# A hybrid block on one core: x also as its transpose, the norm moved behind the projections, two chunks streamed first

## The chip, the cores and the metric

The kernel runs on 1 core of a Trainium2 chip. The metric is the device time of one execution in microseconds. A core has a matmul engine (TensorE, PE in the rows; its weight loads are PEld), a vector engine (VectorE, DVE), an activation engine (ScalarE, ACT), a general engine (GpSimd, POOL) and a queue that issues all transfers of this kernel (SyncE, SPq). Each runs its own list of instructions in order, and semaphores tie the lists together.

## The reference, cut to what matters

```
h = rmsnorm(x, g_mix_pre)                    # x: 1024 tokens x 1024; per token 1/rms, per column g
proj = h @ w_in                              # qa ka va gate (4 heads x 128), beta alpha (4+4), qb kb vb (8 heads x 64)
out_a = gated_deltanet(...)                  # conv over tokens, silu, l2norm; per chunk of 64 tokens
                                             #   t_inv = inverse(I + a), then a recurrence over chunks
out_b = dilated_attention(qb, kb, vb, rel_bias)
x = x + rmsnorm(concat(out_a, out_b) @ w_out, g_mix_post)
h = rmsnorm(x, g_ffn_pre)
out = x + rmsnorm((silu(h @ w_gate) * (h @ w_up)) @ w_down, g_ffn_post)
```

All arrays are float32. Since rmsnorm scales a token by one number r, `(x * r * g) @ w` is `r * ((x * g) @ w)`.

## The kernel before

The work is written as strands (Python generators, one for each task). A recording layer, the Weaver, runs them against its own table of costs and writes the instructions of each engine in the order in which they come up; every instruction therefore has the line of that one call, L267, and rows are read by tiles and shapes. On the chip the order is fixed and each engine waits where its operands are late.

A float32 product is made of three matmuls in a faster 32-bit form: both operands are split into a high part (a cast) and a low part (the rest), and `mm3` adds hi·hi, hi·lo and lo·hi in one PSUM bank. So every operand costs a cast (mostly ACT) and a subtraction (mostly DVE) before PE can use it.

Stage one (to about 300 us) works as follows. `norm_in` (L1171) loads a tile `xt` of 128 tokens, squares it on ACT with a sum (`junk`, `ss`), forms r on DVE and POOL (`n_m`, `n_r`), scales the tile by r and g on DVE, transposes it on PE (8 transposes into banks `tp`, 64 in all) and splits the result into `hTh` and `hTl`, the transposed activations. `load_w` (L625) loads the weight chunks `wr` of `w_in` in the sequence of `ORDER` (two transfers of 256 KB for a chunk of 128 columns), and `prep_w` splits them into `w`. `main` (L1132) is the strand of the projections and has the lowest priority: what it does fills PE whenever nothing else is due. Its first item is bv0 (`proj_v`, vb of four heads with beta and alpha: per token tile 24 matmuls of 264 columns, 192 in all), then k0, q0, k1 and so on: `proj_half` makes 24 matmuls of 512 columns for half of the tokens into one of two banks `pj`, and a sink reads the bank out and gives it back. `raw_sink` (L1110) copies k, q and v to `raw` on ACT. From there `post_k`, `post_q` and `post_v` do the convolution (four DVE passes, `yc`) and the rest, `intra` (L954) the products of a head inside its chunks (`pm<-kq` on PE, two groups of 64-column matmuls per head), `inverse` the triangular inverses by 31 steps on DVE, and `solve` (L1073), once per head, finishes them with four groups of small matmuls on PE (`pm<-uz`, `pm<-B,zz`, twice `pm<-attnT,B`). There are two banks `pm`.

After that come the recurrence and the attention with the last projections between them (300 to 500 us), the output projection `pw` (to about 640 us) and the feed-forward part (`bank`).

Of the kernel before, what the change touches and what calls it, by code (L numbers as in the profile page):

```python
# [21 lines left out]
P = 128  # L22
# [24 lines left out]
AHEAD = 2  # L47
SWITCH = 170.0
BREATH = 200.0
ORDER = "bv0,k0,q0,k1,q1,k2,q2,k3,q3,bq0,bv1,bk0,v0,v1,v2,v3,bq1,bk1,bq2,bk2,bq3,bk3,gate0,gate1,gate2,gate3"  # L50
# [471 lines left out]
def block_kernel(ctx: ExitStack, tc: tile.TileContext, a, out):  # L522
# [77 lines left out]


# [23 lines left out]
    def load_w():  # L625
        for item in order:
            for c in chunks(item):
                z = []
                for i in range(2):
                    wr = yield rawS.get([P, 4, P], F32, name="wr")  # L630
                    yield SY.dma_start(wr[:], a["w_in"][c][:, 4 * i:4 * i + 4, :])
                    z.append(wr)
                w.spawn(prep_w(c, z), 1)
            ev_w0.fire()

    ev_w0 = Event()

    def prep_w(c, raw):
# [7 lines left out]
        for i, (wr, wh, wl) in enumerate(zip(raw, hi, lo)):  # L646
# [11 lines left out]
        wts[c] = hi, lo  # L658
        loaded[c].fire()

# [11 lines left out]
    def proj_qk(c0, m, ev):  # L672
        scale = 0.125 if c0 == 16 else None
# [15 lines left out]
    def proj_v(m):  # L689
# [6 lines left out]
        def sink(t, ps):  # L696
            vs = yield outS.get([P, 4, 2, 64], F32R, name="vs")
            yield from split(vs[:, :, 0, :], vs[:, :, 1, :], ps[:, 0:256].rearrange("p (h d) -> p h d", h=4))
            if not m:
                yield A.copy(bp[:, :, t], ps[:, 256:WB])  # L700
            pj.put(ps)
# [3 lines left out]
        evs = []  # L705
        for t in range(NT):
            yield ev_ht[t]
            ps = yield pj.get([P, n], F32, name="pj")
# [10 lines left out]
            evs.append(w.spawn(sink(t, ps), 1))  # L719
        if not m:  # L720
            w.spawn(beta_alpha(evs), 2)
    def gate(*hs):
        def sink(h, hf, ps):
            z = yield gstS[h // 2, hf].get([P, 512], F32, name="gst")
            yield Either(A.copy(z[:], ps[:]), V.tensor_copy(z[:], ps[:]))
# [40 lines left out]
    ev_ht = [Event() for _ in range(NT)]  # L766
# [28 lines left out]
    def load_consts():  # L795
        yield ev_ht[3]
# [156 lines left out]

    def intra(h):  # L954
# [5 lines left out]
        for i, (m_in, lhs) in enumerate(((mD, trir), (mDT, tgtr))):  # L960
            rh = yield pk.get([P, 2 * NT, 64], F32R, name="rhd", bufs=1)
            yield G.tensor_tensor(rh[:], g2[:, h, :].bitcast(F32).unsqueeze(2).broadcast_to([P, 2 * NT, 64]),
                                  m_in[:].unsqueeze(1).broadcast_to([P, 2 * NT, 64]), ALU.mult)
# [12 lines left out]
            yield G.tensor_tensor(dst, dst, m_in[:].unsqueeze(1).broadcast_to([P, NT, 64]), ALU.mult)  # L976
# [6 lines left out]
        kq = kqs[h]  # L983
        for b in range(2):
            yield After(kq[:])
            kk = yield pm.get([P, 4, 2, 64], F32, name="pm")
            ops = []
# [4 lines left out]
            yield ops  # L992
# [27 lines left out]
    def inverse(evs):  # L1020
# [46 lines left out]
        for q in range(4):  # L1067
            w.spawn(solve(q, a21, uz, B, gs), 3, MARGIN, PACE)

    ev_g_out = [Event() for _ in range(GH)]  # L1070
    ev_gs = {(q, b): Event() for q in range(GH) for b in range(2)}

    def solve(q, a21, uz, B, gs):  # L1073

        sl = slice(q * 8, q * 8 + 8)
        yield After(a21[:], uz[:], B[:])
        zp = yield pm.get([P, 8, 32], F32, name="pm")
        yield [mm(zp[o:o + 32, u, :], a21[o:o + 64, q * 8 + u, :], uz[o:o + 64, q * 8 + u, :])
               for u in range(8) for o in (0, 64)]
        zz = yield pv.get([P, 8, 64], F32, name="zz", bufs=2)  # L1080
        yield G.memset(zz[:], 0.0)
        for o in (0, 64):
            yield V.tensor_tensor(zz[o:o + 32, :, 32:64], zp[o:o + 32, :, :],
                                  rk[o:o + 32, q, :].unsqueeze(2).broadcast_to([32, 8, 32]), ALU.mult)
        pm.put(zp)
        t2 = yield pm.get([P, 8, 32], F32, name="pm")
        yield [mm(t2[o:o + 64, u, :], zz[o:o + 32, u, :], B[o:o + 32, q * 8 + u, 0:32])
               for u in range(8) for o in (0, 64)]
# [3 lines left out]
        for b in range(2):  # L1092
            gg = yield pm.get([P, 4, 2, 64], F32, name="pm")
            ops = []
            for k in range(4):
                u = q * 8 + b * 4 + k
                for c in range(2):
                    o = c * 64
                    r = attnT[o:o + 64, u, :, :]
                    ops.append(mm(gg[o:o + 64, k, :, :], B[o:o + 64, u, :], turned(r) if c else r))  # L1100
            yield ops
            if q:
                yield ev_gs[q - 1, b]
            yield A.copy(gs[:, b], gg[:].rearrange("p t c j -> p t (c j)"))
            pm.put(gg)
            yield SY.dma_start(d_g[4 * b:4 * b + 4, :, q, :].rearrange("t p d -> p t d"), gs[:, b])
            ev_gs[q, b].fire()
        ev_g_out[q].fire()

    def raw_sink(raw):  # L1110
        def sink(hf, ps):
            yield A.copy(raw[0][:, 3 + hf * 512:3 + hf * 512 + 512], ps[:])
            pj.put(ps)
# [18 lines left out]
    def main():  # L1132
        fin = []
        for n, (kind, i) in enumerate(order):
            if n == 1:
# [1041 lines left out]
```

## Time and profile before

| | |
|---|---|
| median of 3 runs | 1289.85 us (1288.58 to 1290.29) |
| the profiled execution | 1291.07 us, of which the span from the first to the last instruction is 1289.1 us |
| PE busy | 1260.2 us of the span, 6654 matmuls |
| DVE, ACT, POOL busy | 974.5, 597.7, 187.8 us |

Busy time is the time in which an engine had an instruction in it. Matmuls overlap their neighbours, so a row of PE gives a duration that is longer than the step from one start to the next; the steps are what PE's time is made of. The waits, and the starts of rows that follow each other, show more than busy shares.

### The profile page before, as it was taken

The numbers are of one execution on the slowest core, as the hardware profiler recorded it, in microseconds if no ns is written. First come the engines' busy times: TensorE is split into PE (matmuls) and PEld (weight loads), VectorE is DVE, ScalarE is ACT, GpSimd is POOL, SyncE is SP. The second block draws the span as 40 slices with busy tenths as digits, with TensorE's granted clock in tenths as the row PEclk, the third lists the DMA queues.
The fourth block names the chain that finished last, engine by engine and source line by source line (L and its number), as shares of the span: only waits on it lengthen the run. The fifth ranks groups of instructions, "written<-read, shape, count | busy, mean of one in ns | idle before, by whom it ended". The sixth has DMA issues, their size and how long they took to land.

```text
span 1289.1 us, 19374 instructions
## 1 busy us (share of the span) xinstructions
PE 1260.2 (98%) x6654; PEld 1044.4 (81%) x6654; DVE 974.5 (76%) x1899; ACT 597.7 (46%) x1216; POOL 187.8 (15%) x168
## 2 busy tenths in 40 slices
PE   6999999999999999999999999999999999999996
PEld 6877798778888888777878888888888888888885
DVE  7688959535897879966698788766787766876875
ACT  5345532224777767744563333333333334544541
POOL 1034430101221202101110011101011100000002
PEclk9999999999999999999999999999999999999999
DMA  7323263649976767577452443223332038734335
GB/s 259 93 75 115 99 198 121 153 152 301 274 241 202 224 198 201 176 238 235 155 167 96 139 156 130 74 98 123 123 110 100 29 131 305 249 125 153 98 114 196
DMA packets 156273, 207.12 MB, mean 161 GB/s; under 512 B 28256, under 2 KB 75616, under 8 KB 156176
## 3 DMA queue, kind: packets, MB, share of 16 engines
q1 hardware_dynamic: 156176, 205.89, 50.2%
q8 instruction: 53, 0.87, 0.3%
q14 instruction: 44, 0.36, 0.1%
HBM read 143.67 MB, written 62.16 MB: 160 GB/s over the span
## 4 chain that ended last, share of the span: by engine, by line
PE 87%; DVE 5%; DMA 4%; ACT 2%; issue 1%; SPq 0%; POOL 0%; DVEq 0%; POOLq 0%; ACTq 0%
PE bank L267 47%; PE pj L267 24%; PE pw L267 4%; PE tp L267 3%; PE p L267 3%; PE pm L267 2%; PE pS L267 2%; PE pV L267 2%; DMA gt<-d_gt 1%; DMA d_mix<-ptmp 1%; DVE x L267 1%; DMA mx<-d_mix 1%; DVE pt L267 0%; DMA d_mix<-ot 0%; DMA xt<-in_x 0%
## 5 line engine op out<-in xcount | busy, mean ns | idle before, releaser
L267 PE MATMUL pj<-hTh,w 128*128 128x512 f32 x768 | 267.3, 403 | 0.0
L267 ACT CAST wbh<-wraw 128x512 fp32r<-128x512 f32 x129 | 79.9, 622 | 201.8 <-PE bank L267 132.7
L267 PEld LDWEIGHTS pj<-hTh,w 128*128 128x128 f32 x768 | 144.4, 188 | 34.5 <-issue 4.2
L267 PE MATMUL pj<-hTl,w 128*128 128x512 f32 x384 | 151.3, 394 | 0.0
L267 DVE TENSOR_TENSOR wbl<-wraw,wbh 128x512 fp32r<-128x512 f32 x132 | 92.6, 704 | 32.5 <-ACT wbh L267 32.4
L267 PEld LDWEIGHTS pj<-hTl,w 128*128 128x128 f32 x384 | 72.5, 189 | 12.0
L267 PE MATMUL bank<-views 128*128 128x512 f32 x284 | 81.6, 391 | 0.0
L267 PE MATMUL bank<-views,dah 128*128 128x512 f32 x216 | 77.3, 394 | 0.0
L267 PE MATMUL bank<-dbh,views 128*128 128x512 f32 x208 | 75.6, 393 | 0.0
L267 POOL TENSOR_TENSOR m<-m,m 128x512 f32<-128x512 f32 x18 | 28.4, 1576 | 279.0 <-DVE r L267 206.8
L267 DVE TENSOR_TENSOR pt<-tp,pt 128x256 fp32r<-128x256 f32 (+1 forms) x160 | 58.7, 389 | 6.3 <-ACT pt L267 4.7
L267 PEld LDWEIGHTS bank<-views 128*128 128x128 f32 x284 | 53.3, 188 | 11.8
L267 ACT ACTIVATE Sr<-Sr,mx 128x128 f32<-128x128 f32 (+3 forms) x64 | 49.4, 773 | 15.9 <-DVE mx L267 15.4
L267 DVE CUSTOM_DVE_ANT_0 Sr<-pS,strip 128x384 f32<-128x384 f32 (+3 forms) x96 | 50.8, 550 | 7.5 <-PE pS L267 4.9
L267 DVE TENSOR_TENSOR w<-wr,w 128x512 fp32r<-128x512 f32 x50 | 36.8, 740 | 25.6 <-ACT w L267 25.2
L267 PE MATMUL pw<-woh,mh 128*128 128x512 f32 x128 | 52.6, 411 | 0.0
L267 PE MATMUL pS<-ks,qs 128*128 128x384 f32 (+3 forms) x192 | 48.7, 357 | 1.8 <-DMA qs<-d_q 1.6
L267 PE MATMUL pw<-woh,ml 128*128 128x512 f32 x128 | 50.5, 394 | 0.0
L267 PE MATMUL bank<-dbh,dah 128*128 128x512 f32 x128 | 50.4, 394 | 0.0
L267 PE MATMUL pw<-wol,mh 128*128 128x512 f32 x128 | 50.4, 393 | 0.0
L267 ACT CAST pt<-tp 128x256 fp32r<-128x256 f32 (+1 forms) x121 | 40.1, 352 | 20.1 <-PE tp L267 12.7
L267 PE MATMUL pj<-w,hTh 128*128 128x264 f32 (+1 forms) x256 | 49.0, 292 | 0.0
(369 smaller groups left out, 3296.9 us busy)
## 6 DMA issues: line engine op xcount, KB each, us to landing
wr<-in_w_in SPq DMA_DIRECT2D x56, 256.0 KB, 3.2
wraw<-in_w_gate SPq DMA_DIRECT2D x52, 256.0 KB, 3.1
wraw<-in_w_up SPq DMA_DIRECT2D x52, 256.0 KB, 2.9
views<-d_hid SPq DMA_DIRECT2D x47, 256.0 KB, 2.9
db<-in_w_down SPq DMA_DIRECT2D x40, 256.0 KB, 4.0
qs<-d_q SPq DMA_DIRECT2D x64, 128.0 KB, 4.7
da<-d_hid SPq DMA_DIRECT2D x30, 256.0 KB, 3.0
d_hid<-x SPq DMA_DIRECT2D x22, 256.0 KB, 3.5
```

The lines of the kernel that those rows point to most:

```text
L267: op.fn(*op.args, **op.kw)
```

## The change

Five things change in stage one; the rest of the program is the same code.

1. The host hands over `x_t`, x transposed, beside x. `load_xt` loads 128 columns of 512 tokens, and `prep_xt` multiplies by g and splits (one ACT, one DVE instruction) straight into `hTh` and `hTl`. r is no longer in them. The 64 transposes, the scaling on DVE and their splits go.
2. r goes to the outputs. `norm_in` still loads x in token tiles, for the squares, and keeps r in `rtok`. Two groups of four PE matmuls spread r of 512 tokens over all partitions (`rb`). Sinks multiply by `rb` or by a column of `rtok`: k, q, v and gate on DVE (before: a copy on ACT, for two gate halves on DVE), bq and bk by a product on DVE and then both splits, bv as the scale of instructions that it had.
3. `ORDER` begins with k0 and q0. `proj_first` runs both together, k step by k step, as weights and `x_t` land: 48 matmuls of 512 columns for the first half of the tokens, then bv0 for four token tiles, then the second half in the same manner. bv0 accumulates in the banks `pt`.
4. `intra` issues the two groups of a head together, and `solve` takes two heads: its groups on PE go from 16 to 8, those of `intra` from 8 to 4, with the same matmuls in all.
5. The masks and outer products in `intra`, on POOL before, may go to DVE or POOL; 5 of 8 outer products and 6 of 8 masks come to DVE.

```diff
-ORDER = "bv0,k0,q0,k1,q1,k2,...
+ORDER = "k0,q0,bv0,k1,q1,k2,...
...
     def load_w():
...
+        first = chunks(order[0]) + chunks(order[1])
...
+        for i in range(2):
+            for n, c in enumerate(first):
+                wr = yield rawS.get([P, 4, P], F32, name="wr")
+                yield SY.dma_start(wr[:], a["w_in"][c][:, 4 * i:4 * i + 4, :])
...
+                if not i:
+                    w.spawn(prep_w(c, got[c], evs[c]), 1)
+                yield from load_xt(4 * i + n, 0)
+                if not i and not n:
+                    yield SY.dma_start(gT[:], a["g_mix_pre_t"])
+            for k in (2, 3):
+                yield from load_xt(4 * i + k, 0)
+        yield SY.dma_start(wba[:], a["w_ba"])
+        yield from load_item(order[2])
+        yield SY.dma_start(ident[:], a["c_ident"])
+        for t in range(4):
+            yield from load_x(t)
+        for k in range(KT):
+            yield from load_xt(k, 1)
+        for t in range(4, NT):
+            yield from load_x(t)
...
+    def proj_first(hf, sinks):
+        cs = chunks(order[0]) + chunks(order[1])
...
+        for k in range(KT):
+            for c, z in zip(cs, ps):
+                yield ev_wh[c, k // 4]
+                yield ev_xt[k, hf]
+                wh, wl = wts[c]
+                yield mm3(z[:], wh[k // 4][:, k % 4, :], wl[k // 4][:, k % 4, :], *h_of(k, hf * 512, 512),
+                          k == 0, k == KT - 1)
...
     def proj_qk(c0, m, ev):
...
-            yield from split(hi[:], lo[:], flip(ps[:]) if c0 == 16 else ps[:], scale)
+            if c0 == 16:
+                yield V.scalar_tensor_tensor(tmp, flip(ps[:]), 0.125, flip(f), ALU.mult, ALU.mult)
+            else:
+                yield V.tensor_tensor(tmp, ps[:], f, ALU.mult)
             pj.put(ps)
+            yield from split_sb(hi[:], lo[:], tmp)
...
     def intra(h):
...
-            yield G.tensor_tensor(rh[:], ...
+            yield Either(*[e.tensor_tensor(rh[:], ...) for e in (V, G)])
...
-        for b in range(2):
-            yield After(kq[:])
+        yield After(kq[:])
+        kks, ops = [], []
+        for b in range(2):
             kk = yield pm.get([P, 4, 2, 64], F32, name="pm")
...
-            yield ops
+        ev_kk[h].fire()
+        yield ops
...
-        for q in range(4):
+        for q in range(0, GH, 2):
             w.spawn(solve(q, a21, uz, B, gs), 3, MARGIN, PACE)
...
-    def raw_sink(raw):
+    def raw_sink(raw, early=False):
         def sink(hf, ps):
-            yield A.copy(raw[0][:, 3 + hf * 512:3 + hf * 512 + 512], ps[:])
-            pj.put(ps)
+            z, f = raw[0][:, 3 + hf * 512:3 + hf * 512 + 512], rb[:, hf * 512:hf * 512 + 512]
+            if early:
+                yield A.copy(z, ps[:])
+                pj.put(ps)
+                yield ev_rb[hf]
+                yield Either(*[e.tensor_tensor(z, z, f, ALU.mult) for e in (V, G)])
+            else:
+                yield V.tensor_tensor(z, ps[:], f, ALU.mult)
+                pj.put(ps)
...
+        def load_xt(k, hf):
+            x = yield px.get([P, 512], F32, name="xT", bufs=6)
+            yield SY.dma_start(x[:], a["x_t"][k, :, hf * 512:hf * 512 + 512])
+            done_in.append(w.spawn(prep_xt(k, hf, x), 1))
+
+        def prep_xt(k, hf, x):
+            yield After(x[:], gT[:])
+            hi, lo = (z[:, k % 4, :] for z in hT[k // 4, hf])
+            f = gT[:, k:k + 1]
+            yield A.activation(hi, x[:], AF.Copy, scale=f)
+            yield V.scalar_tensor_tensor(lo, x[:], f, hi.bitcast(F32), ALU.mult, ALU.subtract)
...
+        def norm_in(t, x):
...
             yield A.activation(junk[:], x[:], AF.Square, accum_out=ss[:])
...
+            yield G.tensor_tensor(rtok[:, t:t + 1], m[:], mhalf[:, 0:1], ALU.pow)
...
+                yield [mm(tp[:, i, :], rtok[:, t - 3 + i:t - 2 + i].broadcast_to([P, P]), ident[:]) for i in range(4)]
+                yield A.copy(rb[:, (t - 3) * P:(t + 1) * P], tp[:].rearrange("p k j -> p (k j)"))
```

How this moves the first transfers on SP, before (`xt` are tiles of 128 tokens, 512 KB; `wr` half chunks of weights, 256 KB, here of bv0 and k0):

```order
L267 DMA xt<-in_x 128x1024
L267 DMA gb<-in_g_mix_pre 128x1024
L267 DMA ident<-in_c_ident 128x128
L267 DMA wba<-in_w_ba 128x64
L267 DMA xt<-in_x 128x1024
L267 DMA wr<-in_w_in 128x512 x4
L267 DMA xt<-in_x 128x1024 x3
L267 DMA wr<-in_w_in 128x512 x4
```

And with the change (`xT` are pieces of the transpose, 256 KB; the first four `wr` rows are k0 and q0, the run of four is bv0; `xn` are token tiles):

```order
L266 DMA wr<-in_w_in 128x512
L266 DMA xT<-in_x_t 128x512
L266 DMA gT<-in_g_mix_pre_t 128x8
L266 DMA wr<-in_w_in 128x512
L266 DMA xT<-in_x_t 128x512 x3
L266 DMA wr<-in_w_in 128x512
L266 DMA xT<-in_x_t 128x512
L266 DMA wr<-in_w_in 128x512
L266 DMA xT<-in_x_t 128x512 x3
L266 DMA wba<-in_w_ba 128x64
L266 DMA wr<-in_w_in 128x512 x4
L266 DMA ident<-in_c_ident 128x128
```

Twelve pieces of 256 KB now stand ahead of bv0, and the token tiles follow behind it.

The first matmuls on PE, before (buffer numbers kept; `tp` are transposes of two token tiles, `pj` is the bank of bv0's first tile):

```order
L267 MATMUL tp_191<-ident_62,xt_149 128x128 x4
L267 MATMUL tp_205<-ident_62,xt_149 128x128 x4
L267 MATMUL tp_224<-ident_62,xt_150 128x128 x4
L267 MATMUL tp_248<-ident_62,xt_150 128x128 x4
L267 MATMUL pj_258<-w_166,hTh_97 128x264
```

And with the change (`pj_152` is k0's bank, `pj_153` q0's; `w_157` and `w_158` are the high and low part of k0's first half):

```order
L266 MATMUL pj_152<-hTh_99,w_157 128x512
L266 MATMUL pj_152<-hTl_100,w_157 128x512
L266 MATMUL pj_152<-hTh_99,w_158 128x512
L266 MATMUL pj_153<-hTh_99,w_168 128x512
L266 MATMUL pj_153<-hTl_100,w_168 128x512
L266 MATMUL pj_153<-hTh_99,w_169 128x512
```

PE begins with a projection whose k step needs one piece of `x_t` and half a chunk of each weight, and no transposes stand in its list. Later in PE's list, in both programs, what is left of the projections surrounds the groups of `solve`; before (`pm_2489` to `pm_2522` are groups of one head each):

```order
L267 MATMUL pm_2489<-uz_1933,a21_2341 32x32 x16
L267 MATMUL pj_2452<-hTh_99,w_2356 128x512
L267 MATMUL pj_2452<-hTl_100,w_2356 128x512
L267 MATMUL pj_2452<-hTh_99,w_2357 128x512
L267 MATMUL pj_2517<-hTh_101,w_2354 128x512
L267 MATMUL pj_2517<-hTl_102,w_2354 128x512
L267 MATMUL pj_2517<-hTh_101,w_2355 128x512
L267 MATMUL pm_2490<-uz_1933,a21_2341 32x32 x16
L267 MATMUL tp_2527<-ident_62,ys_2495 128x128 x4
```

And with the change:

```order
L266 MATMUL pm_2531<-uz_1911,a21_2384 32x32 x32
L266 MATMUL pj_2496<-hTh_101,w_2399 128x512
L266 MATMUL pj_2496<-hTl_102,w_2399 128x512
L266 MATMUL pj_2496<-hTh_101,w_2400 128x512
L266 MATMUL pj_2578<-hTh_103,w_2397 128x512
L266 MATMUL pj_2578<-hTl_104,w_2397 128x512
L266 MATMUL pj_2578<-hTh_103,w_2398 128x512
L266 MATMUL pm_2532<-uz_1911,a21_2384 32x32 x32
L266 MATMUL tp_2587<-ident_62,ys_2572 128x128 x4
```

A group now has twice the matmuls and there are half as many. Counted over both lists, the only changes in kind on PE are the 64 transposes less and 8 matmuls `tp<-ident,rtok` more. From the transposes of `y3` in the output projection on, the order on every engine is the same as before: on PE these are the last 2899 of 6075 matmuls, on DVE the last 783 of 1916 instructions, on ACT the last 448 of 1086.

## Rows read from the trace of the kernel before

**Rows 1.** The page, busy time of each engine: us (share of the span) x instructions.

```profile
PE 1260.2 (98%) x6654; PEld 1044.4 (81%) x6654; DVE 974.5 (76%) x1899; ACT 597.7 (46%) x1216; POOL 187.8 (15%) x168
```

**Rows 2.** What PE waited for, 0 to 40 us: us in total, times, longest.

```profile
PE tp L267 <- DVE xt L267: 11.0, 2, 7.8
```

**Rows 3.** The same from 300 to 640 us: first and last of five rows.

```profile
PE pS L267 <- DMA qs<-d_q: 1.6, 1, 1.6
...
PE pS L267 <- DVE oss L267: 0.2, 1, 0.2
```

**Rows 4.** Timeline of PE at the start: start us, us, engine, line, operation.

```profile
7.79 1.97 PE L267 MATMUL tp<-ident,xt 128*128 128x128 f32 x8 [7.79 <-DVE xt L267]
...
12.97 1.97 PE L267 MATMUL tp<-ident,xt 128*128 128x128 f32 x8 [3.21 <-DVE xt L267]
...
16.05 0.64 PE L267 MATMUL pj<-w,hTh 128*128 128x264 f32 x2
...
16.50 0.42 PE L267 MATMUL pj<-w,hTl 128*128 128x264 f32 x1
...
17.97 0.41 PE L267 MATMUL pj<-w,hTh 128*128 128x264 f32 x2
...
18.21 0.28 PE L267 MATMUL pj<-w,hTl 128*128 128x264 f32 x1
```

**Rows 5.** The chain that ended last, pieces in order of time: start us, us, what.

```profile
22.20 0.87 PE tp L267 x8
23.07 1.47 PE pj L267 x12
...
37.27 12.87 PE pj L267 x84
...
73.59 9.07 PE pj L267 x39
...
303.39 0.89 PE p L267 x8
```

**Rows 6.** Timeline of PE around a group of 64-column matmuls.

```profile
87.84 0.60 PE L267 MATMUL tp<-ident,kq 128*128 128x128 f32 x4
88.37 1.09 PE L267 MATMUL pm<-kq 128*64 128x128 f32 x16
89.40 0.50 PE L267 MATMUL pj<-hTh,w 128*128 128x512 f32 x1
89.74 0.39 PE L267 MATMUL pj<-hTl,w 128*128 128x512 f32 x1
```

**Rows 7.** Transfers of weights: on the page (KB each, us to landing), and SP's timeline.

```profile
wr<-in_w_in SPq DMA_DIRECT2D x56, 256.0 KB, 3.2
...
3.06 2.20 SPq L267 DMA_DIRECT2D wr<-in_w_in  x4
```

**Rows 8.** Busy time by stretch; the last two numbers are DMA share and GB/s.

```profile
10.00:20.00 10.00, 7.03 (x43) 7.03 (x44) 9.10 (x17) 6.85 (x16) 3.36 (x6) 1.00 0.90 323
```

**Rows 9.** Groups of instructions, 0 to 30 us: busy us, mean ns of one.

```profile
L267 DVE SCALAR_TENSOR_TENSOR xt<-xt,n_r,gb 128x1024 f32<-128x1024 f32 x7 | 8.9, 1278 | 0.7 <-POOL n_r L267 0.7
...
L267 DVE TENSOR_TENSOR w<-wr,w 128x512 fp32r<-128x512 f32 x6 | 4.0, 686 | 0.0
...
L267 ACT CAST w<-wr 128x512 fp32r<-128x512 f32 x6 | 3.6, 611 | 0.0
```

**Rows 10.** Busy time by stretch (PE, PEld, DVE, ACT, POOL), and groups from 40 to 300 us.

```profile
60.00:200.00 140.00, 140.00 (x819) 114.68 (x817) 109.46 (x180) 63.99 (x91) 50.61 (x31) 1.00 0.38 121
200.00:300.00 100.00, 100.00 (x762) 79.06 (x761) 58.23 (x100) 25.82 (x41) 6.85 (x11) 1.00 0.54 155
...
L267 DVE SCALAR_TENSOR_TENSOR yc<-raw,convw,yc 128x1024 f32<-128x1024 f32 x36 | 46.8, 1301 | 0.6
...
L267 DVE TENSOR_TENSOR bl<-pj,bh 128x512 fp32r<-128x512 f32 x4 | 2.7, 686 | 5.7 <-ACT bh L267 5.7
...
L267 ACT COPY raw<-pj 128x512 f32<-128x512 f32 x24 | 14.0, 584 | 38.2 <-PE pj L267 38.0
```

More of the change, by code (lines that the diff above doesn't have):

```diff
@@ L599, in block_kernel @@
     onorm = pgv.tile([P, 1], F32, name="onorm")
+    rtok = pgv.tile([P, NT], F32, name="rtok")
+    rb = pgv.tile([P, S], F32, name="rb")
+    ev_r = [Event() for _ in range(NT)]
+    ev_rb = [Event() for _ in range(2)]
     wp = pool(ctx, "wp", 1, side="right")
@@ L625, in load_w, with load_item, prep_w @@
     def load_w():
[L626 to L638, printed above, removed]
+        first = chunks(order[0]) + chunks(order[1])
+        got = {c: [] for c in first}
+        evs = {c: [Event() for _ in range(2)] for c in first}
+        for i in range(2):
+            for n, c in enumerate(first):
+                wr = yield rawS.get([P, 4, P], F32, name="wr")
+                yield SY.dma_start(wr[:], a["w_in"][c][:, 4 * i:4 * i + 4, :])
+                got[c].append(wr)
+                evs[c][i].fire()
+                if not i:
[14 more added lines that the diff above has]
+            yield from load_x(t)
+        ev_x.fire()
+        for item in order[3:]:
+            yield from load_item(item)
+    def load_item(item):
+        for c in chunks(item):
+            z, evs = [], [Event() for _ in range(2)]
+            for i in range(2):
+                wr = yield rawS.get([P, 4, P], F32, name="wr")
+                yield SY.dma_start(wr[:], a["w_in"][c][:, 4 * i:4 * i + 4, :])
+                z.append(wr)
+                evs[i].fire()
+            w.spawn(prep_w(c, z, evs), 1)
+    ev_x = Event()
+    ev_wh = {(c, i): Event() for c in loaded for i in range(2)}
+    def prep_w(c, raw, got):
         hi, lo = [], []
@@ L645, in prep_w @@
             (lo if i % 2 else hi).append(z)
-        for i, (wr, wh, wl) in enumerate(zip(raw, hi, lo)):
+        wts[c] = hi, lo
+        for i, (wh, wl) in enumerate(zip(hi, lo)):
+            yield got[i]
+            wr = raw[i]
             if c in (24, 25):
@@ L704, in sink @@
             ev_v[m][t].fire()
[L705 to L708, printed above, removed]
+        for t in tiles:
+            if m:
+                bank = ps = yield pj.get([P, n], F32, name="pj")
+            else:
+                bank = yield pt.get([P, 4, P], F32, name="tp")
+                ps = bank[:].rearrange("p k j -> p (k j)")[:, 0:n]
             for k0 in range(0, KT, 2):
@@ L718, in proj_v @@
                     wS.put(wh, wl)
-            evs.append(w.spawn(sink(t, ps), 1))
-        if not m:
-            w.spawn(beta_alpha(evs), 2)
+            w.spawn(sink(t, ps, bank), 1)
+        if not m and tiles[-1] == NT - 1:
+            w.spawn(beta_alpha(ev_v[0]), 2)
     def gate(*hs):
@@ L952, in post_q @@
         ev_kq[h].fire()
+    ev_kk = [Event() for _ in range(GH)]
     def intra(h):
@@ L1133, in main @@
         fin = []
+        pair = []
+        for _ in range(2):
+            raw = yield from new_raw()
+            pair.append((raw, []))
+        for hf in range(2):
+            evs = yield from proj_first(hf, [raw_sink(raw, True) for raw, _ in pair])
+            for (_, ev), e in zip(pair, evs):
+                ev.append(e)
+            yield from proj_v(0, range(4 * hf, 4 * hf + 4))
+        ev_v0.fire()
         for n, (kind, i) in enumerate(order):
-            if n == 1:
-                yield loaded[base[kind] + i]
-                wS.slots = wS.slots[:8]
             if kind in ("k", "q", "v"):
-                raw, ev = (yield from new_raw()), []
-                for hf in range(2):
-                    e = yield from proj_half(base[kind] + i, hf, raw_sink(raw))
-                    ev.append(e)
-                if n == 1:
-                    ev_v0.fire()
+                if n < 2:
+                    raw, ev = pair[n]
+                else:
+                    raw, ev = (yield from new_raw()), []
+                    for hf in range(2):
+                        e = yield from proj_half(base[kind] + i, hf, raw_sink(raw))
+                        ev.append(e)
                 if kind == "k":
@@ L1187, in norm_in @@
                 pt.put(tp)
-            px.put(xt)
-            ev_ht[t].fire()
+                ev_rb[t // 4].fire()
         w.spawn(issue(V.memset(mhalf[:], -0.5)), 0)
-        wS.more(px, "pw", 4)
-        done_in = [w.spawn(norm_in(t), 1) for t in range(NT)]
+        wS.more(px, "pw", 8)
         w.spawn(load_w(), 2)
```

147 lines of the change are left out of this document (89 added, 58 removed).

## The prediction

> **What bounds the kernel now.** I read the busy times first, then PE's waits, then starts that follow each other. PE had an instruction in it for 98% of the span [rows 1], and the steps between starts show that this is real work: in the middle of stage one 39 matmuls of 512 columns take 9.07 us, 0.2326 us each [rows 5], and nothing stands between them. So work taken out of PE's list, or a wait of PE taken away, comes off the end, as long as no new wait replaces it. The reader is to see three places where PE loses time.
>
> The first is the start. PE's first instruction is at 7.79 us and after eight transposes it is idle again until 12.97; the waits for the scaled tile `xt` sum to 11.0 us [rows 2, 4]. A second loss hides in the steps: two matmuls of 264 columns take 0.45 us from 16.05 to 16.50, but 0.24 us from 17.97 to 18.21 [rows 4]. That is 0.22 against 0.12 us for one, the ratio of the two clock levels, 1.2 and 2.4 GHz, although the granted clock in the row of that stretch reads 1.00 [rows 8]. PE had worked without a gap since 12.97 when the step fell. The whole loss follows from the end of bv0. A transpose takes 0.87 / 8 = 0.109 us and a matmul of 264 columns 1.47 / 12 = 0.1225 [rows 5]. The 84 matmuls in 12.87 us from 37.27 are 60 of bv0 (7.35 us) and 24 of k0 (5.58 us), so bv0 ends at 37.27 + 7.35 = 44.6. At the upper level its 192 matmuls and the 64 transposes are 23.5 + 7.0 = 30.5 us. Lost: 14.1 us, 11.0 of it waits and 3.1 the lower clock.
>
> The second place is small: each group of 64-column matmuls costs something to enter and leave. Four transposes before one take 0.53 us from start to start instead of 4 x 0.109 = 0.44, and the matmul behind it 0.34 instead of 0.23 [rows 6], together 0.20 us. The third are the waits between 300 and 640 us, 4.6 us in five rows [rows 3]. From the transposes of `y3` on, order and work are unchanged, so that part takes as long as now and I charge it nothing.
>
> **The change, part by part.**
>
> *Transposes and broadcasts.* 64 x 0.109 = 7.0 us leave PE's list. The 8 matmuls that spread r are plain float32 of 128 columns; rows of that kind (`p`, four instructions shown as x8, 0.89 us [rows 5]) take 0.22 us each, so 1.8 us come in. Net -5.2.
>
> *The start.* SP issues a 256 KB load every 2.20 / 4 = 0.55 us, and such a load lands in 3.2 us [rows 7]. The first weight half is issued at about 0.7 and lands at 3.9; the cast takes 0.61 and the subtraction 0.69 [rows 9], so 5.2 us; the first piece of `x_t`, one issue later, has its high part at about 5.1. PE's first matmul needs the two high parts: 5.2 us. Twelve pieces feed the first 48 matmuls. On DVE each costs 0.64 (half of the 1278 ns row) to 0.69 us [rows 9], about 8 us in all, from 4.5 to 12.5; by DMA 3.1 MB at 323 GB/s [rows 8] are 9.7 us. PE needs 48 x 0.2326 = 11.2 us at the upper level and 22.3 at the lower. It is the slowest of the three at either, so it doesn't starve once it runs. What it spends at the lower level no row shows; the bounds are nothing and all 48 matmuls. I take the 3.1 us that it cost before, since then too PE went over after an unbroken run of work. The first half of k0 and q0 then ends at 5.2 + 11.2 + 3.1 = 19.5, and 8.3 us are lost instead of 14.1: -5.8, with bounds of -8.9 (no lower level) and +2.2 (5.2 + 22.3 = 27.5, 16.3 lost).
>
> On this the Trainium skill speaks against the change: "TensorE: Matmul & The Clock Gate", section "Loop structure matters more than you think", has a loop that waits for a DMA at every step as the bad pattern, since TensorE then stays at the lower clock. By it the whole first half runs at the lower clock and the term is the upper bound, +2.2. The rows agree that waiting PE is slow (it idled from about 9.8 to 12.97 and the matmuls behind were at 0.22 us); whether PE will wait here no run shows.
>
> What must hold behind it: bv0's four weight pieces are issued as `wr` buffers come free, the last at about 11, landing near 15. But on ACT the last cast stands behind the copy of k0's bank, which waits for k0's last matmul at 18.8: 18.8 + 0.58 + 0.61 + 0.69 = 20.7. PE asks for it after 18 of 24 matmuls of the first tile, 19.5 + 2.2 = 21.7. Hidden by 1.0 us; without that cover it costs that excess once. The matmuls that spread r stand in bv0's fourth tile, at 19.5 + 3 x 2.94 + 0.7 = 29.0. The fourth token tile reuses a buffer, so SP holds its load until the first square is done (about 21.4); with 256 KB more than a weight piece it lands at 21.4 + 3.2 + 0.8 = 25.4, and square, DVE, POOL and the hops between them need some 2.5 us: 28. Cover 1 us, cost if gone 1 to 2 us. Behind that blocked load SP also holds the second half of `x_t`, needed only from 32 us on. I charge nothing.
>
> *Groups.* 16 to 8 in `solve`, 8 to 4 in `intra`: 12 x 0.20 = -2.4 us. The matmuls are the same. Between 0 (the cost is in the matmuls' shape after all) and -4.1 (a group of 16 takes 1.03 us, 0.14 more than 16 x 0.055 would be if two share the array; saving that too).
>
> *Sinks on DVE.* 20 reads of `pj` at 0.58 us leave ACT and come to DVE at about 0.69 [rows 10]: 13.8 us; 15 extra subtractions for bq and bk 10.4; 6 gate halves 4.1; 5 outer products of twice the length about 6; masks net of other moves 2.1; back come 8 weight subtractions and 3 copies, -7.6. About +29 us on DVE between 45 and 500 us, where between 60 and 300 alone it has 72 us free (30.5 + 41.8 [rows 10]). It costs nothing while a sink comes within the 5.6 us in which PE fills the other bank (24 x 0.2326). A convolution, the longest thing ahead of it, is three passes of 1.30 and one shorter [rows 10], under 5 us. So I take nothing; the bound is the slow rival below. Below nothing it can't go: no row shows PE waiting for ACT's copies.
>
> *300 to 640 us.* The order is planned anew, the projections run out sooner and `pw` fills in for them. The 4.6 us of waits may go or double; I take no change.
>
> **Sum.** -5.2 - 5.8 - 2.4 = -13.4 us: the profiled execution (1289.1 span, 1291.07 in all) becomes 1277.7. It lies 1.2 above the median of the runs shown, so I predict 1276.4 for the median.
>
> **The rivals.**
>
> *A, the streamed half stays at the lower clock:* the head start is eaten, start term +2.2, sum -5.4, 1284.4 us. For it: the first transposes had no lasting effect on the clock [rows 4]. Against: at the lower level a k step keeps PE busy for 2.6 us, while DVE delivers one about every 1.0.
>
> *B, the middle waits:* attention ends later in PE's new list (67 us of PE work stand behind its last matmul, 86 before), so there is less to cover `d_mix` and its loads. Doubled waits: +4.6, 1281.0 us. Against: 67 us is still much.
>
> *C, DVE holds `pj` (slower):* a sink is a DVE instruction now and DVE serves in order. If convolutions of two chunks stand ahead of it (9 us), PE finds both banks full. If each of the 20 halves loses 1.0 us: +20, sum +6.6, 1296.5. It decides against the change from 0.67 us per half. For it: DVE was 78% busy from 60 to 200 us. Against: the 72 us above.
>
> *D, more than forecast:* no lower clock (-3.1) and most of the middle waits gone (-3.3): 1270.0; with the groups at their bound 1.7 less still.
>
> **How the numbers follow.** Chances: the forecast, 1272 to 1282 with the unknown sizes, 0.60; D 0.10; A 0.10; B 0.08; C 0.08; A and B together, no change that can be told, 0.04. The range from 1269 to 1285 leaves out C, the pair and the ends of D: not quite 2 in 10. The runs shown lie within 0.13%, so 0.2% (2.6 us) is what can be told from no change. A and B alone are faster by more than that. A mild form of C, near 0.67 us per half, is no change: I give the same 0.05, of it 0.04 the pair, slower 0.07, and faster 0.88.
>
> **What would show it.** The start: PE's first matmul near 5 us, steps of 0.43 us falling to 0.23 before about 13 us, bv0 beginning between 18 and 21; waits of PE before 40 us under 7 instead of 11. Transposes: no `tp<-ident,xt`. Groups: 4 and 8 groups with the same edges of about 0.1 us. DVE: no wait of PE `pj` for DVE `raw`. The shift is then whole by about 260 us and stays to the end. I am wrong if the steps stay at 0.43 through k0 and q0, if PE's waits from 60 to 300 us come to several us, or if those from 300 to 640 us exceed 9.

## The result, and the profile after

The changed kernel takes 1274.1 us at the median (1271.83 to 1275.21), the kernel before 1290.07 in the same comparison; the ratio is 0.9859 with a 95% interval of 0.9840 to 0.9878, 16 to 18 us less. Forecast were 1276.4 and a range of 1269 to 1285. The profiled execution took 1273.72 us with a span of 1271.9, which is 17.2 less than before; the working said 13.4. So 3.8 us more came than the sum has, and they are the interesting part.

The page of the kernel after, busy time of each engine (compare [rows 1]): 48 matmuls fewer, and DVE busy about as long as before.

```profile
PE 1249.3 (98%) x6606; PEld 1039.9 (82%) x6606; DVE 980.2 (77%) x1914; ACT 587.9 (46%) x1196; POOL 201.1 (16%) x175
```

PE's timeline at the start, after (start us, us, engine, line, operation, idle before and what ended it; compare [rows 4]):

```profile
5.10 0.80 PE L266 MATMUL pj<-hTh,w 128*128 128x512 f32 x1 [5.10 <-ACT hTh L266]
...
9.04 1.05 PE L266 MATMUL pj<-hTh,w 128*128 128x512 f32 x2
...
10.32 1.05 PE L266 MATMUL pj<-hTh,w 128*128 128x512 f32 x2
...
14.21 0.62 PE L266 MATMUL pj<-hTh,w 128*128 128x512 f32 x2
...
14.89 0.62 PE L266 MATMUL pj<-hTh,w 128*128 128x512 f32 x2
...
19.20 0.41 PE L266 MATMUL tp<-w,hTh 128*128 128x264 f32 x2
...
28.67 1.05 PE L266 MATMUL tp<-ident,rtok 128*128 128x128 f32 x8
29.48 0.49 PE L266 MATMUL tp<-w,hTh 128*128 128x264 f32 x2
```

The first matmul stands at 5.10 us (forecast 5.2). From 9.04 to 10.32 three matmuls take 1.28 us, 0.427 each; from 14.21 to 14.89 three take 0.68, 0.227 each: the lower and the upper level again, while the granted clock of both stretches reads 1.00 (third number from the end), as in [rows 8]:

```profile
0.00:10.00 10.00, 4.90 (x11) 3.44 (x12) 4.01 (x9) 5.71 (x8) 0.20 (x4) 1.00 0.78 251
10.00:20.00 10.00, 10.00 (x46) 8.30 (x45) 6.89 (x15) 6.96 (x16) 0.00 (x0) 1.00 0.92 333
```

That 1.00 is no reading at the start: the trace's record of the granted clock begins only at 11.3 us here and at 17.0 us in the kernel before, and the view counts time without a record as 1.00. Both are the moments at which the steps fall.

The first half of k0 and q0 ends at 19.20 (forecast 19.5), and there is no idle time in it. The spread of r stands at 28.67 (forecast 29.0) and costs 0.81 us.

What PE waited for after the start, three rows from 40 to 300 us and then five from 300 to 640 us (us in total, times, longest; compare [rows 3]):

```profile
PE tp L266 <- POOL rtok L266: 0.6, 1, 0.6
PE tp L266 <- DVE kn L266: 0.4, 1, 0.4
PE tp L266 <- ACT ys L266: 0.3, 1, 0.3
...
PE pS L266 <- DVE pt L266: 2.0, 1, 2.0
PE tp L266 <- DVE y L266: 1.4, 1, 1.4
PE pV L266 <- DVE gst L266: 0.4, 1, 0.4
PE pS L266 <- DVE mx L266: 0.2, 1, 0.2
PE tp L266 <- DVE ptmp L266: 0.2, 1, 0.2
```

No row names `pj` waiting for a sink on DVE. The waits from 300 to 640 us are 4.2 us in five rows, 4.6 before. The wait for `y` among them, 1.4 us, has its like before the change at 652 us, 1.5 us and outside those 4.6; so up to the last transposes of `y` 6.1 us of waits became 4.2. The tail is the same: the last transpose of `y` starts at 656.1 us before and at 638.8 after, which leaves 633.0 and 633.1 us to the end of the span.

The chain of work of a quiet stretch, where nothing but projections runs on PE (start us, us, what); first before, then after:

```profile
198.32 21.72 PE pj L267 x94
```

```profile
185.88 22.21 PE pj L266 x98
```

21.72 / 94 is 0.2311 us for one matmul, 22.21 / 98 is 0.2266. These are the same instructions on operands of the same shapes; the change doesn't touch them, and still each is 4.5 ns shorter. The missing microseconds can be there. The experiments go after it first, then after the terms of the sum.

### The profile page after: what moved, and what is told of

The parts are those of the page before. It is cut to its first block, busy times and chain, and to the rows that moved or that the text cites. A ratio compares the mean times of both kernels' runs of the same rounds, so it can differ in the third digit from the quotient of the medians.

```text
span 1271.9 us, 19295 instructions
## 1 busy us (share of the span) xinstructions
PE 1249.3 (98%) x6606; PEld 1039.9 (82%) x6606; DVE 980.2 (77%) x1914; ACT 587.9 (46%) x1196; POOL 201.1 (16%) x175
## 4 chain that ended last, share of the span: by engine, by line
PE 89%; DVE 6%; DMA 3%; issue 1%; ACT 1%; POOL 0%; SPq 0%; DVEq 0%; POOLq 0%; ACTq 0%
PE bank L266 48%; PE pj L266 20%; PE pw L266 6%; PE tp L266 4%; PE p L266 3%; PE pS L266 3%; PE pV L266 2%; PE pm L266 2%; DMA xn<-in_x 1%; PE rp L266 1%; DVE x L266 1%; DMA xT<-in_x_t 0%; DMA qs<-d_q 0%; DVE h2r L266 0%; DMA h2l<-d_h 0%
## 5 line engine op out<-in xcount | busy, mean ns | idle before, releaser
L266 PE MATMUL pj<-hTh,w 128*128 128x512 f32 x768 | 264.6, 402 | 5.1 <-ACT hTh L266 5.1
L266 ACT ACTIVATE Sr<-Sr,mx 128x384 f32<-128x384 f32 (+4 forms) x64 | 49.4, 773 | 13.1 <-DVE mx L266 12.6
L266 ACT CAST w<-wr 128x512 fp32r<-128x512 f32 x53 | 32.4, 618 | 43.0 <-PE pj L266 35.3
L266 PEld LDWEIGHTS bank<-views,dah 128*128 128x128 f32 x216 | 40.6, 188 | 9.2
```

What stands on the lines that cost most here:

```text
L266: op.fn(*op.args, **op.kw)
```

## The experiments

In the built programs one thing about these operands does differ: where the tiles lie in SBUF. Before, bv0 comes first in `ORDER` and its weight tiles, 2 x 264 numbers or 2112 bytes per partition, take the eight buffers `w` that the program keeps. After, k0 and q0 take them, with 4 x 128 numbers or 2048 bytes. So before, the rows of weights lie at every distance from the rows of `hTh` and `hTl` that 2112 makes (counted within 256 bytes these are 0, 64, 128 and 192, about a quarter of the projections each), and after, every row of weights starts at the same byte as the rows of `hTh` and `hTl`, counted within 512. I had two theories: the **layout** sets the step, or the **load** of the other engines does (it changed with the new order). Four kernels, pad64, shift64, b2176 and b2304, move tiles alone. Every engine's list of instructions is the same as in the kernel that each is made from. The runs come from several sittings, in which the kernel before took 1290.07 to 1292.92 us at the median; ratios to it therefore compare better than times.

**again**: the changed kernel once more, as the base.

> The changed kernel itself, as the base for the three that follow. 1274 us, 16 less than before; in the stretch from 186 to 208 us, where nothing but projections runs on PE, 24 matmuls of 512 columns take 5.44 us, as in its first profile.

Measured: 1274.22 us, ratio 0.9866 (0.9845 to 0.9888).

**pad64**: 64 unused bytes at the low end of SBUF.

```diff
+    pc.tile([P, 16], F32, name="pad")
     ident = pc.tile([P, P], F32, name="ident")
```

> The changed kernel with one unused tile of 64 bytes ahead of everything at the low end of SBUF; every engine keeps its order. With it all 2772 matmuls of the feed-forward part have moving rows and weight rows that start at the same byte within 128 (812 and 476 of them had before, 1484 had not). Theory, layout: their mean step falls from 0.2295 us towards the 0.227 to 0.2285 of the aligned projections: 3 to 7 us less, 1269 us, all of it behind 620 us. Rival, order and load: 1274 us, nothing moves.

Measured: 1269.19 us, ratio 0.9821 (0.9801 to 0.9840); its interval lies wholly under that of the run before it. 5.0 us less for 64 bytes that nothing reads. The chain of the feed-forward part from 700 us on, the changed kernel and then pad64:

```profile
699.91 30.17 PE bank L266 x132
```

```profile
699.83 30.37 PE bank L266 x134
```

0.2286 us for one becomes 0.2266. In 200 us from 800 on PE does 885 matmuls instead of 876, as the busy time by stretch says (the changed kernel, then pad64):

```profile
800.00:1000.00 200.00, 200.00 (x876) 164.20 (x875) 145.58 (x211) 66.66 (x114) 24.02 (x16) 1.00 0.30 98
```

```profile
800.00:1000.00 200.00, 200.00 (x885) 165.58 (x884) 147.07 (x213) 67.11 (x115) 23.91 (x16) 1.00 0.30 98
```

The load theory had nothing moving. It falls here.

**shift64**: `hTh` and `hTl` 64 bytes lower.

```diff
+    ph = pool(ctx, "ph", 1, side="right")
-    hS = Slots(pool(ctx, "ph", 1, side="right"), "ph", 8)
+    hS = Slots(ph, "ph", 8)
     hT = {...}
+    ph.tile([P, 16], F32, name="pad")
```

> The changed kernel with an unused tile of 64 bytes behind hTh and hTl, so that these lie 64 bytes lower and no projection has its moving rows and its weight rows at the same byte within 128; every engine keeps its order. Theory, layout: 24 projections in the quiet stretch near 200 us take 5.55 to 5.60 us instead of 5.44, stage one ends some 4 us later; the feed-forward part, where the shift makes 2424 of 2772 equal, takes 2 to 5 us less; the sum is near nothing, 1272 to 1278. Rival, order and load: no stretch changes by more than 0.5 us.

Measured: 1275.72 us, ratio 0.9873 (0.9855 to 0.9891). The sum is near nothing as expected, and the parts go as the layout theory has them: in the quiet stretch 96 projections take 22.40 us, 0.2333 each, the slowest of the quiet stretches shown here, and the feed-forward part has 880 matmuls in the same 200 us.

```profile
188.81 22.40 PE pj L266 x96
```

**b2176**: the kernel before, its weight buffers at a pitch of 2176 bytes, 17 x 128.

```diff
-                z = yield wS.get([P, 2, WB], F32R, name="w")
+                z = yield wS.get([P, 2, WB + 8], F32R, name="w")
...
```

> The kernel before with only the eight buffers of the split weights moved: their pitch is 2176 bytes instead of 2112, so that all rows of weights and all rows of hTh and hTl start at the same byte within 128; every engine keeps its order. Theory, the layout of SBUF sets the step: the mean step of the 512-column projections falls from 0.232 to about 0.228 us, 24 of them in the quiet stretch near 200 us from 5.55 to 5.44 us, and 1152 times 0.0035 is 4 us: 1286 us. Rival, the step fell in the changed kernel because the order or the load on other engines changed: 1290 us, steps as before.

Measured: 1293.41 us, ratio 1.0001 (0.9988 to 1.0015): nothing. The chain near 200 us:

```profile
197.96 22.19 PE pj L267 x96
```

0.2311 each, as before. So my form of the theory was wrong: equal within 128 bytes isn't enough. With this pitch nearly half of the weight rows are 128 bytes off the rows of `hTh` within 256. All aligned matmuls of the changed kernel and of pad64 are equal within 256 as well. With the addresses of the built program laid beside PE's starts, 191 of 955 steps in this run go from one projection that is equal within 256 to another; their median is 0.227 us, that of the others 0.231 to 0.233. An operand that is off costs the step beside it too, so half of the rows aligned is worth next to nothing.

**b2304**: the same with a pitch of 2304 bytes, 9 x 256 (`WB + 24` in the line above).

> The kernel before with the buffers of the split weights at a pitch of 2304 bytes, nine times 256; every engine keeps its order. With a pitch of 2176 bytes half of the rows were equal to hTh and hTl within 128 bytes but not within 256, and their steps stayed at 0.232 to 0.235 us; now 1104 of 1152 projections and all 384 matmuls of the output projection are equal within 256. Theory, layout with a period of 256 bytes: 24 projections in the quiet stretch near 200 us take 5.44 us as in the changed kernel, and 1104 times 0.0035 and 384 times 0.0035 are 5 us: 1285 to 1287 where the kernel before has 1290 to 1292. Rival, what set the step in the changed kernel isn't the layout of the weights: no change.

Measured: 1289.27 us, ratio 0.9976 (0.9962 to 0.9990).

```profile
196.78 22.44 PE pj L267 x99
```

22.44 / 99 is 0.2267, the step of the changed kernel, in the order of the kernel before. With that the layout is shown from both sides: made worse in the changed kernel, made good in the one before. The time fell by 1.3 to 4.9 us where I expected 5; over all projections the mean step between PE's records fell from 0.2319 to 0.2295 only, in part since 48 of the 1152 are still not equal, in part since the step settles anew after each interruption: by the starts in PE's records the first step of an unbroken run of projections is 0.234 us on the mean and from the eleventh on 0.227, and there are 197 such runs here, 179 in the changed kernel.

**rev**: is streaming what the start gained?

```diff
-        for k in range(KT):
+        ks = range(KT) if hf else range(KT - 1, -1, -1)
+        for k in ks:
...
-                          k == 0, k == KT - 1)
+                          k == ks[0], k == ks[-1])
```

> The changed kernel with the k steps of the first half of k0 and q0 in reverse, 7 to 0: the same matmuls, but the first of them needs the piece of the transpose that lands last, so nothing streams. Theory, streaming is what the start gained: PE begins near 13 us instead of 5.1, the half ends at 13 + 11.2 + up to 3.1 for the lower clock, near 26 instead of 19.2, and the time is 5 to 8 us longer, 1279 to 1282. Rival, what the start gained comes from the transposes alone and the head start is eaten by the weights of bv0 or by the spread of r: within 2 us of 1274.

Measured: 1283.96 us, ratio 0.9923 (0.9902 to 0.9944), 8 us over the changed kernel by the ratios and 10 by the medians, more than the 5 to 8 expected. PE's timeline:

```profile
14.05 0.79 PE L266 MATMUL pj<-hTh,w 128*128 128x512 f32 x1 [14.05 <-ACT hTh L266]
...
18.84 0.63 PE L266 MATMUL pj<-hTl,w 128*128 128x512 f32 x1
19.27 0.78 PE L266 MATMUL pj<-hTh,w 128*128 128x512 f32 x2
19.88 0.39 PE L266 MATMUL pj<-hTl,w 128*128 128x512 f32 x1
20.11 0.62 PE L266 MATMUL pj<-hTh,w 128*128 128x512 f32 x2
...
27.82 0.41 PE L266 MATMUL tp<-w,hTh 128*128 128x264 f32 x2
```

PE begins 8.9 us later, the half ends 8.6 later, and all of it reaches the end. Here too PE is at the lower level first (18.84 to 19.27 is 0.43 us) and at the upper soon after (19.88 to 20.11 is 0.23), though all pieces have landed. The lower level belongs to PE's beginning after it stood idle, not to streaming.

**warm**: ten matmuls on zeros while PE waits for its first operands.

```diff
+WARM = 10
...
+        def warm():
+            z = hT[1, 1][0][:, 0, :]
+            yield V.memset(z.bitcast(F32), 0.0)
+            bank = yield pt.get([P, 4, P], F32, name="tp")
+            o = bank[:].rearrange("p k j -> p (k j)")
+            yield [mm(o, z[:, 0:P], z) for _ in range(WARM)]
+            pt.put(bank)
+        w.spawn(warm(), 0)
```

> The changed kernel with ten matmuls of 512 columns on zeros ahead of PE's list, into a bank that is written anew later; 4.3 us of work at the lower level, in the 5.1 us in which PE waits for its first operands. Theory, the 3.1 us that the first 14 projections lose at 0.427 us are a matter of PE's clock and come back when it has worked before them: the half ends up to 3 us sooner, at 16 to 17.5, and the time falls by 1 to 3 us. Rival, the pieces of the transpose bound the half (DVE is busy without a gap from 10 to 15 us): it ends at 18 to 19 as before, the time within 0.7 us of the changed kernel's.

Measured: 1275.11 us, ratio 0.9855 (0.9835 to 0.9876): the same as without. PE's timeline, one of its waits up to 60 us, and then rows behind that wait, with the busy time of the stretch (third number from the end is the granted clock):

```profile
6.66 0.63 PE L267 MATMUL pj<-hTh,w 128*128 128x512 f32 x2
7.12 0.40 PE L267 MATMUL pj<-hTl,w 128*128 128x512 f32 x1
...
17.93 0.41 PE L267 MATMUL tp<-w,hTh 128*128 128x264 f32 x2
```

```profile
PE tp L267 <- POOL rtok L267: 2.3, 1, 2.3
```

```profile
47.40 0.60 PE L267 MATMUL tp<-w,hTh 128*128 128x264 f32 x2
...
50.65 0.51 PE L267 MATMUL tp<-w,hTh 128*128 128x264 f32 x2
...
47.00:51.00 4.00, 4.00 (x23) 4.00 (x22) 3.47 (x5) 1.85 (x4) 1.35 (x1) 0.57 0.80 193
```

The third and fourth real matmuls take 0.46 us together (6.66 to 7.12), 0.23 each, so the lower level is all but gone, and the half ends at 17.93, 1.3 us sooner. But the second spread of r now waits 2.3 us for `rtok` instead of 0.6, and behind this wait PE is at the lower level once more: the 15 matmuls of 264 columns from 47.40 to 50.65 take 0.217 us each where 0.12 is usual, and the granted clock of the stretch reads 0.57. That is 1.7 and 1.4 us, so the 1.3 us gained turn into 1.9 us lost in this profile. The rival's result came by another road: not the pieces, but the token tiles that were loaded last, and the clock behind them. Whether the clock fell in the executions without a profile isn't known.

**best**: pad64, eight matmuls on zeros, and the last four token tiles loaded between the pieces of the second half.

```diff
         for k in range(KT):
             yield from load_xt(k, 1)
-        for t in range(4, NT):
-            yield from load_x(t)
+            if k % 2:
+                yield from load_x(4 + k // 2)
```

> The changed kernel with what the runs suggest: the tile of 64 bytes at the low end of SBUF (1269.2 us by itself), eight matmuls on zeros ahead of PE's list, and the last four token tiles loaded between the pieces of the second half of the transpose, since with the warm-up alone the half ended 1.3 us sooner and the wait for rtok near 45 us took 1.7 us more. If that wait was what took the gain, 1267; if the gain is lost to the next thing that is late, 1269.

Measured: 1270.12 us, ratio 0.9819 (0.9799 to 0.9838), not to be told from pad64 alone. The wait for `rtok` is gone, and up to 490 us PE is 1.8 to 2.0 us ahead of where pad64 has it. All of that is lost in one place. It isn't the waits: from 300 to 640 us they are 7.5 us here and 6.7 in pad64, among them the same 2.01 us for `pt` in both. It is what follows this wait, first in best, then in pad64 (each with the busy time of the stretch around it):

```profile
496.88 1.19 PE L267 MATMUL pS<-ks,qs 128*128 128x512 f32 x2 [2.01 <-DVE pt L267]
...
499.28 1.52 PE L267 MATMUL rp<-ident,psums 128*64 128x128 f32 x16
...
503.52 0.39 PE L267 MATMUL pw<-woh,mh 128*128 128x512 f32 x1
...
495.00:500.00 5.00, 3.12 (x13) 2.21 (x15) 5.00 (x14) 1.60 (x4) 2.27 (x2) 0.68 1.05 273
```

```profile
498.44 0.70 PE L266 MATMUL pS<-ks,qs 128*128 128x512 f32 x2 [2.01 <-DVE pt L266]
...
503.58 0.39 PE L266 MATMUL pw<-woh,mh 128*128 128x512 f32 x1
...
495.00:500.00 5.00, 2.99 (x16) 1.94 (x16) 5.00 (x13) 2.58 (x6) 1.29 (x2) 1.00 1.05 297
```

The same matmuls take 6.64 us in best and 5.14 in pad64, since in best the clock was at its lower level for part of them (granted clock 0.68). These are single profiles; over the executions best and pad64 are level. So pad64 is the version to keep; the other two edits have shown no gain.

**apart**: solve for each head and the groups of `intra` as before, the rest as changed.

```diff
-        for q in range(0, GH, 2):
+        for q in range(4):
             w.spawn(solve(q, a21, uz, B, gs), 3, MARGIN, PACE)
...
```

> The changed kernel with solve once per head and the two groups of intra apart, as in the kernel before: 16 and 8 groups on PE instead of 8 and 4, the planner orders stage one anew around them. Theory, every group costs about 0.2 us to enter and leave: 2.4 us more, 1276.5. Rival, the cost is in the shape of the matmuls, not in the groups: no change. A third, a lone group of 16 has the array half empty, too: up to 4.1 more.

Measured: 1280.48 us, ratio 0.9888 (0.9868 to 0.9907), about 3 us over the changed kernel by the ratios and 6 by the medians. The time alone doesn't put the rival with no change out: the interval overlaps that of the changed kernel, and the planner's new order brings waits of its own (6.2 us from 300 to 640 us, 4.2 in the changed kernel). What merging is worth is read from rows. A merged group in the changed kernel:

```profile
106.90 0.40 PE L266 MATMUL pj<-hTh,w 128*128 128x512 f32 x1
107.23 1.97 PE L266 MATMUL pm<-kq 128*64 128x128 f32 x32
109.13 0.50 PE L266 MATMUL pj<-hTh,w 128*128 128x512 f32 x1
109.47 0.40 PE L266 MATMUL pj<-hTl,w 128*128 128x512 f32 x1
```

It takes 1.90 us for 32, where two groups of 16 took 2 x 1.03 [rows 6]: 0.16 less. Its edges are 0.10 (0.33 for the matmul ahead instead of 0.227) and 0.11 (0.34 behind), and one such pair is saved. 0.16 + 0.10 + 0.11 is 0.37 for each group of this kind that is gone. From start to start, all 24 groups take 23.0 us before and the 12 of the changed kernel 21.4; with about 0.20 for each pair of edges that is gone, 2.4, merging is worth 4.0 us in all.

**sink2**: the late sinks do their multiply twice.

```diff
                 yield V.tensor_tensor(z, ps[:], f, ALU.mult)
+                yield V.tensor_tensor(z, ps[:], f, ALU.mult)
                 pj.put(ps)
```

> The changed kernel with the multiply that reads a bank of k, q or v out done twice in each of the 20 late sinks (and the warm-up of the kernel that carries it, ten matmuls on zeros at the start): 20 times 0.69 us more on DVE, each bank held 0.69 us longer. Theory, DVE has time to spare and the sink is hidden behind the 5.4 us in which PE fills the other bank: within 1 us of the kernel with the warm-up alone. Rival, DVE holds the banks: 10 to 14 us more.

The kernel that ran doesn't have the warm-up after all, so it is compared with the changed kernel. Measured: 1283.38 us, ratio 0.9923 (0.9904 to 0.9942), 7 to 9 us more for 13.8 us of DVE work. Neither theory has this right. PE's waits from 300 to 640 us:

```profile
PE pV L266 <- DVE pt L266: 2.6, 1, 2.6
PE rp L266 <- DVE psums L266: 2.0, 2, 1.2
PE pS L266 <- DMA d_mix<-ptmp: 1.9, 1, 1.9
```

With smaller ones they are 10 us instead of 4.2, and no matmul waits for a bank `pj`. The planner orders the attention anew around the longer sinks, so DVE's load and the new order can't be told apart here.

**sinkpool**: the opposite, the multiply on POOL.

```diff
-                yield V.tensor_tensor(z, ps[:], f, ALU.mult)
+                yield A.copy(z, ps[:])
                 pj.put(ps)
+                yield G.tensor_tensor(z, z, f, ALU.mult)
```

> The changed kernel with the 20 late sinks of k, q and v as a copy on ACT, as before the change, and the multiply by the spread r on POOL: 13.8 us less on DVE; the planner orders stage one and the attention anew. Theory of the prediction, the sinks on DVE cost nothing: within 2 us of 1274. Rival, from the run with the doubled sinks, where 13.8 us more on DVE made the time 9 us longer with PE waiting in the attention: DVE's load counts at some two thirds, so 13.8 us less are up to 9 us less, 1265 to 1272.

Measured: 1278.15 us, ratio 0.9884 (0.9864 to 0.9903), 2 to 4 us over the changed kernel where the rival had up to 9 us less. Taking the sinks off DVE gained nothing, in an order of the attention that is again the planner's own.

## Why the prediction was right, and where its sum was off

| step of the prediction | forecast | what the runs show |
|---|---|---|
| transposes | -7.0 | gone; -7.0 |
| spread of r | +1.8 | twice 0.81 us: +1.6, and a wait of 0.6 |
| start | -5.8 | 19.20 less 48 x 0.227 is 8.3 us lost, 14.1 before: -5.8 |
| groups, 12 fewer | -2.4 | -4.0 |
| sinks on DVE | 0 | no wait of `pj`; moving them off DVE gained nothing |
| waits, 300 to 640 us | 0 | 4.6 became 4.2; up to the last `y` 6.1 became 4.2: -1.9 |
| waits of `kn` and `ys` | 0 | +0.7 |
| lower level behind a wait, 495 us | not in the sum | +1.5, in this profile |
| step of the matmuls that stay | not in the sum | 0.2319 became 0.2287 on the mean: -4.9 at most; b2304 alone: -3.1 |

*The start* came out term by term: first matmul, end of the half, place of the spread of r. The 3.1 us that I took for the lower level, from before and between bounds of nothing and 11 us, were right: the first 14 matmuls take 6.35 us, from 5.10 to 11.45 (rows at the end), where 14 x 0.227 are 3.2. The size holds in other starts too (counted in the same way 2.9 us in rev and 2.5 in again); that it met to 0.1 us is luck. Rival A is out: 34 of the 48 matmuls are at the upper level. The section "Loop structure matters more than you think" of "TensorE: Matmul & The Clock Gate" in the Trainium skill speaks of a loop that waits for a transfer at every step. In this half PE waits for none, so the rule has nothing to act on here. The streaming itself is worth 8 to 10 us, as rev shows.

*The groups* were right in kind and too small. I counted the edges and took the two streams of a group as half empty only for the bound of -4.1. The rows say that the bound was the better value: the edges gave the 2.4 of the sum, and the groups themselves became 1.6 us shorter, since one of twice the matmuls takes less than two.

*The sinks* were right for the reason given, that PE has another bank to fill. But the thought behind it, that DVE has 72 us to spare, need not carry far: with another 13.8 us of the same work the time was 7 to 9 us longer, by the load or by the new order that came with it. The slack of a stretch doesn't say what an engine's load does to the stretch behind it, since here all that follows is planned around it.

*What failed* is a sentence ahead of the sum: that 39 matmuls at 0.2326 us each are real work, with nothing between them. I took that step for a constant of the instruction. It isn't: the same instructions step at 0.2267 us where the tiles lie well, the least seen here, and the difference to 0.2326 is the price of where they lay. The edit to `ORDER` moved them, without a word on it in the diff. The forecast held even so because its range was wider than this term. The mean step from one 512-column matmul of the projections to the next, of all steps under 0.26 us in PE's records behind 20 us, is 0.2319 before (962 steps) and 0.2287 after (931); that of the output projection falls as much. For 1152 + 384 matmuls 0.0032 us each are 4.9, an upper value, since not every matmul has one of its kind behind it. By the run that does this alone to the kernel before (b2304) it is 3.1 us, between 1.3 and 4.9. Taken out of the ratio, 0.9859 / 0.9976, the rest of the change is worth about 15 us, not far from the 13.4 of the sum.

The term of +1.5 us is the clock, as in best. In the profile after, too, PE waits 2.01 us for `pt` and then works at the lower level for a while, which the profile before doesn't have there:

```profile
495.00:500.00 5.00, 5.00 (x26) 3.69 (x27) 4.96 (x14) 3.50 (x5) 2.83 (x2) 0.66 1.02 354
```

From the end of that wait at 495.00 the same matmuls take 6.66 us, and 5.14 in pad64. The terms as measured then add up to -19.2 with 4.9 us for the step, and to -17.4 with the 3.1 of b2304, where the span shows -17.2. So the sum closes within 2 us; which of the terms is too large by that was not traced.

The prediction let all that PE gains come off the end "as long as no new wait replaces it". Most of it did. About 1 us of the start is slack: in the second profile of the changed kernel PE begins 1.6 us later and the half ends 0.9 later, but there the second spread of r doesn't wait for `rtok`, and behind it the two profiles are level (46.56 and 46.60 us). The next 1 to 2 us that warm and best gain were lost to a longer wait for `rtok` and to the clock. The 8.6 us that rev loses at the start reach the end.

## What to carry to other kernels

A step that PE repeats without a gap is not yet the step of the instruction: divide a quiet stretch of the chain by its count, compare it with other stretches of the same shape, and if they differ by some per cent look at the addresses of the tiles before looking at the engines. A change that alters which tile comes first, or how large a buffer is, can move them all; put the rows that one matmul reads at a multiple of 256 bytes from each other. And before building more on a gain of 1 to 2 us, look in the profile at the next wait that can eat it and at the granted clock behind that wait: one fall of the clock is worth as much.

## What the runs showed of the hardware that I had not expected

- The step of a 512-column matmul depends on the distance in SBUF between the rows that stream and the rows of weights. Equal within 256 bytes: 0.2266 to 0.2267 us (the changed kernel, pad64, b2304). 64 bytes apart: 0.2333 (shift64). At mixed distances, 128 bytes among them: 0.2311 (the kernel before, b2176), and 0.2286 in the feed-forward part of the changed kernel, where equal rows and rows 64 bytes apart alternate. Other distances had no run of their own, and what in the chip makes the difference is open.
- The step isn't at its lowest at once after PE has changed level or kind (0.234 us for the first step of a run of projections, 0.227 from the eleventh on, as said under b2304). In the changed kernel the three matmuls from 14.21 to 14.89 us are at 0.227 each. The three that begin at 11.45, the first at the upper level, take 0.70 us together:

```profile
11.45 0.63 PE L266 MATMUL pj<-hTh,w 128*128 128x512 f32 x2
...
12.15 0.62 PE L266 MATMUL pj<-hTh,w 128*128 128x512 f32 x2
```

- A wait of 2.0 us in the attention was followed by a stretch at the lower clock level in three profiles (the changed kernel, best, and rev with 1.98 us) and not in pad64, with the same matmuls around it: 6.6 to 6.7 us against 5.1.
- The first matmul of the program starts between 5.10 us and, in the second profile of the same kernel, 6.72 us, since its operands landed later.

```profile
6.72 0.79 PE L266 MATMUL pj<-hTh,w 128*128 128x512 f32 x1 [6.72 <-ACT hTh L266]
```
